# Attention scores as 64x64x64 products in the quarters of the array, and state products of two heads side by side

## The chip, the cores and the metric

The kernel runs on one core of one Trainium2 chip. A time is the device time of one execution in microseconds (us). The engines have short names: PE is TensorE (its weight loads are PEld), DVE is VectorE, ACT is ScalarE, POOL is GpSimd, and SP is SyncE, which here issues the DMAs.

## The reference

One layer of a diffusion backbone: a SwiGLU feed-forward with half a residual, a mixer of two head groups, and a second such feed-forward, for 1024 latent tokens and 256 context tokens of width 1024. Nine vectors per sample (adaLN) shift, scale and gate the stages. The change lies in the first head group, a gated linear attention (GLA) over chunks of 64 tokens that runs in both directions:

```python
GLA_HEADS = 4; GLA_DK = 64; GLA_DV = 128; GLA_CHUNK = 64
def step(s, xs):                                  # one chunk; s is the state
    qc, kc, vc, gc = xs
    b = jnp.cumsum(gc, axis=2)
    rel = b[:, :, :, None, :] - b[:, :, None, :, :]
    decay = jnp.exp(jnp.where(lower, rel, -jnp.inf))
    scores = jnp.einsum('bhid,bhjd,bhijd->bhij', qc, kc, decay)
    o = (jnp.einsum('bhij,bhjv->bhiv', scores, vc)
         + jnp.einsum('bhid,bhdv->bhiv', qc * jnp.exp(b), s))
    ...
s, o = lax.scan(step, s0, ...)                    # forwards, and on flipped tokens backwards
```

Each key feature decays on its own, so a score is no plain product of q and k. The second head group is a gated MLP over chunks of 128 positions (`u * (W_s v + b)`). Both groups are joined and go through one output projection.

## The kernel before

**Blocks.** The 1024 latent tokens are two blocks (`tb`) of 512, each of four tiles of 128. The four heads of the GLA have 64 key features each; two heads lie on the 128 partitions, so `dt` (0, 1) counts pairs of heads and `hp` (0, 1) the half of a pair. A half is 64 partitions.

**Scores by levels.** The kernel works with tiles of 128 tokens, not with chunks of 64. For a pair of tokens whose numbers in a tile differ first in bit `l`, the decay splits into a factor of the query and one of the key, taken at a common border. `level` (L1016) makes the scaled queries and keys of one of seven levels for one pair of heads: `sub` (L1027) on DVE, the exponentials (L897) on ACT, and the product with q and k (L1044) on DVE. `scores` (L1047) takes four products of 128 keys with 128 queries over 64 features into one PSUM bank `sc` (L1056). A stage is a level or the diagonal; it has four such banks, and two blocks have eight stages each: 64 banks. ACT copies the diagonal's banks into the tiles `S` (L1069), and for each level a predicated copy on DVE (L1075) writes those places of a bank that a mask of this level names into `S`. A float32 product is two PE instructions in the trace.

**Outputs of the GLA.** `gla_norm` (L1079) adds three products into a bank `o`: `S` with the values (L1095), and the states that come from the left (L1097) and from the right (L1099) with the scaled queries, each over 64 features. Then come the norm's sums (`st`, L265), a spread over partitions (`bc`, L288) and a product (L1113).

**Order.** The mixer (L1260) records the front, the scores of block 0, the scan of the states (`ds`, L1005), the outputs of block 0, the scores of block 1, 48 sums for the adaLN vectors of the next stage (`ada_part`, L158: a DMA of 256 KB into a tile `ar`, of which there are two, and a sum L168 on DVE against a row `cr`), the projections `vs` (L1135 to L1137) and `ogu` (L356 to L359) that `fill` (L1121) makes, the gated MLP (`mix`, L1221), the outputs of block 1, and the output projection (`wo`), whose sums `x<-wo` DVE adds to the stream (L1312). A scheduler sets each engine's order from these, with simulated costs, under the numbers of buffers that the pools have: three banks `po` for `sc`, `ds`, `o` and `mix`, three banks `pg` for projections, 32 tiles `d` (which hold `S`, `cr`, the inputs of the gated MLP and others), seven tiles `h`. So the projections of `fill`, which depend on none of the scores, stand between them on PE.

Of the kernel before, what the change touches and what calls it, by code (L numbers as in the profile page):

```python
# [9 lines left out]
U8 = mybir.dt.uint8  # L10
I32 = mybir.dt.int32
AF = mybir.ActivationFunctionType
ALU = mybir.AluOpType
# [3 lines left out]
P = 128  # L17
# [5 lines left out]
C_BADA, C_N1, C_N2, C_N3, C_FG, C_BG, C_GG, C_CONV, C_END = 0, 72, 80, 88, 96, 104, 108, 109, 181  # L23


class Layer:
# [72 lines left out]

    def mixer_consts(self):  # L100
        nc, a = self.nc, self.a
        b = self.cp.tile([P, 7 * P + 512], U8, name="bytes", tag="bytes")
        self.masks, self.reset = b[:, :7 * P], b[:, 7 * P:]
        nc.vector.tensor_copy(self.masks, self.load(a["masks"], 7 * P)[:, :7 * P])
# [942 lines left out]
    def scores(self, qk, tp, hp):  # L1047

        ps = self.po("sc")
# [7 lines left out]
        return ps.rearrange("p (h i) -> p h i", i=P)  # L1057

    def gla(self, tb):

        nc = self.nc
        hv = lambda t: t.rearrange("p (h i) -> p h i", i=P)
        S = {}
        for hp in range(2):
            t = self.d("S")
            S[0, hp], S[1, hp] = t[:, :512], t[:, 512:]
# [12 lines left out]
    def gla_norm(self, tb, S, qe):  # L1079

        nc = self.nc
        on, sqs = {}, {}
        st = self.pn("st")
        for hp in range(2):
            r = slice(hp * 64, hp * 64 + 64)
            pos = []
            for dt in range(2):
                po = self.po("o")
                for t in range(4):
                    i = 4 * tb + t  # L1090
                    ts = slice(t * P, (t + 1) * P)
                    c = (2 * (t % 2) + dt) * P
                    sf = self.state(2, 1) if i == 0 else self.state((i - 1) // 4, (i - 1) % 4)
                    sb = self.state(2, 0) if i == 7 else self.state((i + 1) // 4, (i + 1) % 4)
                    nc.tensor.matmul(po[:, ts], self.v[tb, 2 * dt + hp][:, ts], S[t // 2, hp][:, c:c + P],  # L1095
                                     start=True, stop=False)
                    nc.tensor.matmul(po[:, ts], sf[r, dt * P:dt * P + P], qe[dt][r, t * P:t * P + P],  # L1097
                                     start=False, stop=False)
                    nc.tensor.matmul(po[:, ts], sb[r, 256 + dt * P:256 + dt * P + P],  # L1099
                                     qe[dt][r, 512 + t * P:512 + t * P + P], start=False, stop=True)  # L1100
                pos.append(po)
            for dt in range(2):
                h = 2 * dt + hp
                sqs[h] = self.h("sq")
                nc.scalar.activation(sqs[h], pos[dt], AF.Square)
                on[h] = S[dt, hp]
                nc.scalar.activation(on[h], pos[dt], AF.Identity, scale=self.par[:, C_GG:C_GG + 1])
                self.col_sums(st, h, sqs[h], 512)
        on, sqs = ([d[h] for h in range(4)] for d in (on, sqs))
        y = self.rstd_cols(sqs, 512, 1.0 / 128.0, None, st)  # L1110
        for h in range(4):
            bc = self.spread(y[:, 4 * h:4 * h + 4], 4)
            nc.vector.tensor_tensor(out=on[h], in0=on[h], in1=bc, op=ALU.mult)  # L1113
        return on


# [123 lines left out]
    def gla_out(self, on, tb):  # L1240
        dst = self.act_tiles()
        for h in range(4):
            og = self.og[h][:, tb * 512:tb * 512 + 512]
            self.nc.vector.tensor_tensor(out=og, in0=og, in1=on[h], op=ALU.mult)
            self.hilo(og, dst[h])
        return dst

# [174 lines left out]
def pack(i):  # L1422
    import numpy as np

    c = np.ascontiguousarray
# [8 lines left out]
    o = {}  # L1434
# [10 lines left out]
    m = np.zeros((P, 7, P), np.float32)  # L1445
    for l in range(7):
        b = np.arange(P) >> l
        m[:, l] = (b[:, None] ^ b[None, :]) == 1
    o["masks"] = m.reshape(P, 7 * P)
# [36 lines left out]
```

## Time and profile before

| | |
|---|---|
| median of three runs | 2215.16 us (2211.38 to 2219.64) |
| profiled execution: its time, its span | 2211.94 us, 2210.2 us |
| PE busy | 2074.9 us, 94% of the span |
| DVE busy | 1560.1 us, 71% |
| ACT busy | 828.6 us, 37% |
| mean granted clock of PE | 0.951 of full speed |

Positions below are us from the start of the span. The mixer's part that the change touches runs from about 1133 (first copy of a diagonal) to 1500 (output projection done); the feed-forwards lie on either side. A busy PE is one whose instructions overlap in the records; it may be at half its clock, which the clock's column tells.

### The profile page before, as it was taken

Reading aid. Unit: us, or ns where it says so; the run is one execution under the profiler, and the core shown is the slowest. Engines: PE = TensorE matmul, PEld = TensorE weight load, DVE = VectorE, ACT = ScalarE, POOL = GpSimd, SP = SyncE. Lnnn points to the kernel's source line nnn. Section 1 sums busy time; section 2 is a strip of 40 time slices with the busy share of each in tenths; the row PEclk is TensorE's granted clock in tenths of the full one; section 3 lists DMA queues with packets and bytes.
Section 4 is the critical chain, followed back from the end, with each engine's and each line's share of the span. In section 5 each row is a group of like instructions: output and inputs, shape, how many; then the busy total and the mean of one; then the engine's idle time right before and its main releaser. Section 6 shows DMA issues by size and latency. Waiting matters only on the chain.

```text
span 2210.2 us, 27546 instructions
## 1 busy us (share of the span) xinstructions
PE 2074.9 (94%) x10308; PEld 1722.6 (78%) x10308; DVE 1560.1 (71%) x2575; ACT 828.6 (37%) x1311; POOL 420.8 (19%) x245
## 2 busy tenths in 40 slices
PE   6799999999999999698999999996999999989995
PEld 2688888888878888577898787775788888867874
DVE  3976566666565689879877267779777776855587
ACT  3633333334351111275444234326344343441222
POOL 0000000000046565232111100110000000065772
PEclk9799999999999999899999986898999999999997
DMA  7033333233469776401111133541334343468851
GB/s 279 34 115 137 121 119 115 115 136 151 153 249 369 272 293 234 156 11 67 39 58 53 68 128 120 181 156 63 144 136 179 123 181 133 179 259 342 304 196 76
DMA packets 115878, 345.05 MB, mean 156 GB/s; under 512 B 12961, under 2 KB 15777, under 8 KB 115745
## 3 DMA queue, kind: packets, MB, share of 16 engines
q1 hardware_dynamic: 115744, 343.30, 42.2%
q8 instruction: 81, 1.33, 0.2%
q14 instruction: 53, 0.43, 0.1%
HBM read 237.87 MB, written 105.38 MB: 155 GB/s over the span
## 4 chain that ended last, share of the span: by engine, by line
PE 72%; DVE 15%; DMA 5%; POOL 3%; issue 3%; ACT 2%; SPq 0%; POOLq 0%; DVEq 0%; ACTq 0%
PE c L479 14%; PE a L479 13%; PE f L479 13%; PE b L479 7%; DVE acc L741 3%; PE sc L1056 2%; PE gc L526 2%; PE gc L525 2%; PE gc L524 2%; DVE acc L512 2%; DMA ar<-in_wb 1%; PE row L205 1%; PE st L265 1%; PE ogu L358 1%; PE ogu L356 1%
## 5 line engine op out<-in xcount | busy, mean ns | idle before, releaser
L384 POOL TENSOR_TENSOR gl<-raw,gh 128x1024 fp32r<-128x1024 f32 x22 | 54.1, 2461 | 1143.9 <-ACT gh L389 1129.6
L389 ACT ACTIVATE gh<-raw 128x1024 fp32r<-128x1024 f32 x66 | 70.0, 1060 | 198.6 <-PE c L479 83.7
L168 DVE SCALAR_TENSOR_TENSOR junk<-ar,cr 128x512 bf16<-128x512 f32 x160 | 111.9, 700 | 35.4 <-DMA ar<-in_wb 26.3
L393 ACT ACTIVATE sh<-s 128x1024 fp32r<-128x1024 f32 x66 | 69.7, 1057 | 170.8 <-PE a L479 93.2
L429 ACT ACTIVATE hl<-g 128x512 fp32r<-128x512 f32 x110 | 67.5, 626 | 158.8 <-DVE g L512 152.2
L479 PE MATMUL f<-hl,uh 128*128 128x512 f32 x528 | 126.8, 389 | 0.0
L479 PE MATMUL c<-hl,sh 128*128 128x512 f32 x352 | 110.9, 392 | 11.4 <-ACT hl L429 9.2
L479 PE MATMUL a<-hl,gh 128*128 128x512 f32 x352 | 113.6, 400 | 8.1 <-ACT hl L429 5.6
L479 PEld LDWEIGHTS f<-hl,uh 128*128 128x128 f32 x528 | 99.1, 188 | 20.6
L479 PE MATMUL b<-hl,gh 128*128 128x512 f32 x352 | 111.5, 393 | 1.0 <-ACT hl L429 1.0
L479 PE MATMUL f<-hl,th 128*128 128x512 f32 x352 | 110.1, 390 | 1.3 <-ACT hl L429 1.3
L479 PE MATMUL a<-hl,sh 128*128 128x512 f32 x352 | 110.2, 393 | 1.0 <-ACT g L552 1.0
L479 PE MATMUL c<-hl,th 128*128 128x512 f32 x352 | 109.0, 391 | 0.1
L741 DVE SCALAR_TENSOR_TENSOR acc<-z,par,acc 128x945 f32<-128x945 f32 (+2 forms) x64 | 95.5, 1511 | 12.0 <-ACT acc L763 10.9
L512 DVE TENSOR_TENSOR u<-c,u 128x512 f32<-128x512 f32 x44 | 30.3, 689 | 98.4 <-ACT u L562 98.4
L430 DVE TENSOR_TENSOR hl<-g,hl 128x512 fp32r<-128x512 f32 x110 | 76.9, 715 | 32.3 <-ACT hl L429 32.2
L142 POOL TENSOR_TENSOR wl<-raw,wh 128x1024 fp32r<-128x1024 f32 x20 | 52.3, 2614 | 222.5 <-ACT wh L141 213.7
L479 PEld LDWEIGHTS c<-hl,sh 128*128 128x128 f32 x352 | 66.2, 189 | 26.7 <-ACT hl L429 9.8
L384 DVE TENSOR_TENSOR sl<-s,sh 128x1024 fp32r<-128x1024 f32 x44 | 53.9, 1224 | 45.7 <-PE gc L525 21.9
L479 PEld LDWEIGHTS a<-hl,gh 128*128 128x128 f32 x352 | 66.6, 193 | 22.1 <-ACT hl L429 6.1
L512 DVE TENSOR_TENSOR acc<-f,acc 128x512 f32<-128x512 f32 x88 | 60.3, 688 | 28.3 <-PE f L479 23.0
L479 PEld LDWEIGHTS b<-hl,gh 128*128 128x128 f32 x352 | 67.0, 190 | 15.7 <-ACT hl L429 1.8
(330 smaller groups left out, 6211.6 us busy)
## 6 DMA issues: line engine op xcount, KB each, us to landing
hd<-hl SPq DMA_DIRECT2D x154, 512.0 KB, 3.7
hc<-hd SPq DMA_DIRECT2D x154, 512.0 KB, 7.7
ar<-in_wb SPq DMA_DIRECT2D x112, 256.0 KB, 3.1
raw<-in_ff1i SPq DMA_DIRECT2D x44, 512.0 KB, 3.8
raw<-in_ff2i SPq DMA_DIRECT2D x44, 512.0 KB, 4.7
raw<-in_ff1o SPq DMA_DIRECT2D x22, 512.0 KB, 6.2
raw<-in_ff2o SPq DMA_DIRECT2D x22, 512.0 KB, 5.4
raw<-in_wa SPq DMA_DIRECT2D x16, 512.0 KB, 10.0
```

The costliest lines, as they stand in the source:

```text
L142: eng.tensor_tensor(out=lo[:, :n], in0=src[:, :n], in1=hi[:, :n].bitcast(F32), op=ALU.subtract)
L168: i = nc.vector.scalar_tensor_tensor(out=self.junk, in0=w, scalar=1.0, in1=cbc[j], op0=ALU.mult, op1=ALU.mult, accum_out=acc[:, h, dt, j:j ...
L384: sub = lambda o, x, y: eng.tensor_tensor(out=o, in0=x, in1=y, op=ALU.subtract)
L389: nc.scalar.activation(gh, g, AF.Copy)
L393: nc.scalar.activation(sh, s, AF.Copy)
L429: nc.scalar.activation(t[:, :512], src, AF.Copy)
L430: nc.vector.tensor_tensor(out=t[:, 512:], in0=src, in1=t[:, :512].bitcast(F32), op=ALU.subtract)
L479: mm = lambda x, y, start, stop: nc.tensor.matmul(ps, x, y, start=start, stop=stop, skip_group_check=more)
L512: tt = lambda eng, o, x, y, op: eng.tensor_tensor(out=o, in0=x, in1=y, op=op)
L524: nc.tensor.matmul(ps, hi[:, c], mh, start=i == 0, stop=False)
L525: nc.tensor.matmul(ps, hi[:, c], ml, start=False, stop=False)
L741: self.nc.vector.scalar_tensor_tensor(out=o, in0=zv[:, r0 + dr:r1 + dr, c0 + dc:c1 + dc], scalar=self.par[:, tap:tap + 1], in1=o, op0=ALU. ...
```

## The change

Scores are taken in 64x64x64 products. Each tile of 128 tokens is cut into halves of 64, and `scores` takes a stage into two banks, one for each `hp`: the keys' half `h` sets the partitions of the bank (the columns of the array) and `hp` the 64 features (its rows), so that four products that follow one another lie in four quarters. A stage has 32 products of four tiles, two pairs of heads, two halves and two `hp`, 64 PE instructions. Levels 0 to 5 and the diagonal stay within a half: they are kept in compact tiles `Sd` of 8 blocks of 64 columns, one for each `hp`. Level 6 holds every pair across the halves; for it the queries' half is swapped, and no mask is needed. Then eight copies on ACT for each block put `S` together, four from level 6's banks and four from `Sd`. Masks shrink to six of 64 columns. In `gla_norm` the loop over `hp` becomes the innermost, so that two state products in the two row halves follow each other. `S` takes its tiles of pool `d` after the last level instead of before the first.

```diff
-        for t in range(2):
+        ps = [self.po("sc") for _ in range(2)]
+        for t in range(4):
             for dt in range(2):
                 q, k = qk[dt]
-                c = slice((2 * tp + t) * P, (2 * tp + t + 1) * P)
-                o = (2 * t + dt) * P
-                self.nc.tensor.matmul(ps[:, o:o + P], k[r, c], q[r, c], start=True, stop=True)
+                o = (2 * t + dt) * 64
+                for h in range(2):
+                    ck, cq = t * P + h * 64, t * P + (1 - h if cross else h) * 64
+                    for hp in range(2):
+                        r = slice(hp * 64, hp * 64 + 64)
+                        self.nc.tensor.matmul(ps[hp][h * 64:h * 64 + 64, o:o + 64], k[r, ck:ck + 64], q[r, cq:cq + 64],
+                                              start=True, stop=True)
...
-        for (tp, hp), St in S.items():
-            ps = self.scores([(self.q[tb, dt], self.k[tb, dt]) for dt in range(2)], tp, hp)
-            nc.scalar.activation(hv(St), ps, AF.Copy, scale=2.0)
-        for l in range(7):
-            qk = [self.level(tb, l, dt) for dt in range(2)]
-            m = self.masks[:, l * P:(l + 1) * P].unsqueeze(1).to_broadcast([P, 4, P])
-            for (tp, hp), St in S.items():
-                ps = self.scores(qk, tp, hp)
-                nc.vector.copy_predicated(hv(St), m, ps)
+            nc.scalar.activation(Sd[hp], ps[hp], AF.Copy, scale=2.0)
+        for l in range(6):
+            ps = self.scores([self.level(tb, l, dt) for dt in range(2)], False)
+            m = self.masks[:, l * 64:(l + 1) * 64].unsqueeze(1).to_broadcast([P, 8, 64])
+            for hp in range(2):
+                nc.vector.copy_predicated(v(Sd[hp]), m, v(ps[hp]))
+        ps = self.scores([self.level(tb, 6, dt) for dt in range(2)], True)
         self.last_level = self.last_exp
+        S = [self.d("S") for _ in range(2)]
+        for hp in range(2):
+            w = S[hp].rearrange("p (n h i) -> p n h i", h=2, i=64)
+            for h in range(2):
+                r = slice(h * 64, h * 64 + 64)
+                nc.scalar.activation(w[r, :, 1 - h], v(ps[hp])[r], AF.Copy)
+                nc.scalar.activation(w[r, :, h], v(Sd[hp])[r], AF.Copy)
         return S
...
-        for hp in range(2):
-            r = slice(hp * 64, hp * 64 + 64)
-            pos = []
-            for dt in range(2):
-                po = self.po("o")
-                for t in range(4):
+        for dt in range(2):
+            pos = [self.po("o") for _ in range(2)]
+            for t in range(4):
...
+                for dr, x in ((0, sf), (1, sb)):
+                    for hp in range(2):
+                        r = slice(hp * 64, hp * 64 + 64)
+                        c = dr * 512 + t * P
+                        nc.tensor.matmul(pos[hp][:, ts], x[r, dr * 256 + dt * P:dr * 256 + dt * P + P],
+                                         qe[dt][r, c:c + P], start=False, stop=dr == 1)
```

How the scheduler orders it shows at three places. The first is PE in the scores of block 0, where the kernel before puts banks of four products (`sc`) between projections (`vs`). Before:

```order
L1135 MATMUL vs_10497<-wh_10409,y_7644 128x256
L1056 MATMUL sc_9123<-x_9109 128x128
L1056 MATMUL sc_9123<-x_9116 128x128
L1056 MATMUL sc_9123<-x_9109 128x128
L1056 MATMUL sc_9123<-x_9116 128x128
L1136 MATMUL vs_10497<-wl_10410,y_7644 128x256
```

Now, the end of the stage in banks 9109 and 9110, and a piece of one of the next stage's banks (9159) behind it:

```order
L1060 MATMUL sc_9109<-x_9102 64x64
L1060 MATMUL sc_9110<-x_9102 64x64
L1145 MATMUL vs_10621<-wl_10618,y_7644 128x256
L1146 MATMUL vs_10621<-wh_10617,y_7648 128x256
L1060 MATMUL sc_9159<-x_9145 64x64 x2
L1060 MATMUL sc_9159<-x_9152 64x64 x2
L1060 MATMUL sc_9159<-x_9145 64x64 x2
L1060 MATMUL sc_9159<-x_9152 64x64 x2
L1060 MATMUL sc_9159<-x_9145 64x64 x2
L1060 MATMUL sc_9159<-x_9152 64x64 x2
L1060 MATMUL sc_9159<-x_9145 64x64 x2
L1060 MATMUL sc_9159<-x_9152 64x64 x2
```

In the first of these stages the two banks alternate, so all four quarters are in turn; in the next only one bank is free, and 16 products of one `hp` run by themselves, in the two column halves of one row half. Of the 16 stages nine go wholly or mostly as the first, seven as the second.

The second place is PE at the end of block 1's scores. Before, the last bank of scores is followed by the outputs:

```order
L1056 MATMUL sc_9994<-x_9962 128x128
L1056 MATMUL sc_9994<-x_9969 128x128
L1095 MATMUL o_11089<-S_9712,v_8484 128x128
L1097 MATMUL o_11089<-b_7871,st_9301 128x128
L1099 MATMUL o_11089<-b_7871,st_9302 128x128
L1095 MATMUL o_11089<-S_9712,v_8484 128x128
```

Now one bank of outputs stands before the last scores, and projections of `fill` behind them:

```order
L1102 MATMUL o_11297<-S_10198,v_8484 128x128
L1108 MATMUL o_11297<-b_7871,st_9407 128x128
L1108 MATMUL o_11297<-b_7871,st_9403 128x128
L1060 MATMUL sc_10165<-x_10157 64x64
L1060 MATMUL sc_10165<-x_10150 64x64 x2
L1060 MATMUL sc_10165<-x_10157 64x64 x2
L358 MATMUL ogu_11161<-y_7646,wh_11157 128x512
L359 MATMUL ogu_11161<-y_7642,wl_11158 128x512
```

In all, 44 instructions of `ogu` that stood before block 1's outputs now stand between them and behind. The state products (now L1108) of two heads stand next to each other in one of four groups of outputs only (block 0, first pair of heads); in the three others one bank follows the other.

The third place is DVE in the output projection, where sums of adaLN (L168) stand between the additions to the stream (L1312, now L1322). Before:

```order
L1312 SCALAR_TENSOR_TENSOR x_11336<-wo_11509,mods,x_11336 128x512
L168 SCALAR_TENSOR_TENSOR junk,acc_10113<-ar_10132,cr_10008 128x512
L1159 TENSOR_TENSOR al_11641<-og_11354,ah_11640 128x512
L1312 SCALAR_TENSOR_TENSOR x_11334<-wo_11528,mods,x_11334 128x512
L1312 SCALAR_TENSOR_TENSOR x_11336<-wo_11542,mods,x_11336 128x512
L168 SCALAR_TENSOR_TENSOR junk,acc_10113<-ar_10135,cr_10008 128x512
L1312 SCALAR_TENSOR_TENSOR x_11338<-wo_11561,mods,x_11338 128x512
```

Now:

```order
L1322 SCALAR_TENSOR_TENSOR x_11536<-wo_11618,mods,x_11536 128x512
L168 SCALAR_TENSOR_TENSOR junk,acc_10270<-ar_10286,cr_10216 128x512
L168 SCALAR_TENSOR_TENSOR junk,acc_10270<-ar_10289,cr_10216 128x512
L1322 SCALAR_TENSOR_TENSOR x_11538<-wo_11637,mods,x_11538 128x512
L168 SCALAR_TENSOR_TENSOR junk,acc_10270<-ar_10292,cr_10216 128x512
L168 SCALAR_TENSOR_TENSOR junk,acc_10270<-ar_10295,cr_10216 128x512
L1322 SCALAR_TENSOR_TENSOR x_11540<-wo_11651,mods,x_11540 128x512
```

The 48 sums need the row `cr`, which now takes its tile of pool `d` after `S`. Before, 34 of them stood ahead of the first addition to the stream, 20 of these among the levels of block 1. Now none stands ahead of the end of these levels, 18 stand between it and the first addition, and 30 behind that, two after each of some 15 additions.

## Rows read from the trace of the kernel before

**Rows 1.** The page: busy time, share and instructions of each engine.
```profile
PE 2074.9 (94%) x10308; PEld 1722.6 (78%) x10308; DVE 1560.1 (71%) x2575; ACT 828.6 (37%) x1311; POOL 420.8 (19%) x245
```
**Rows 2.** The chain that ended last: its shares, then pieces (start, us, what).
```profile
PE 72%; DVE 15%; DMA 5%; POOL 3%; issue 3%; ACT 2%; SPq 0%; POOLq 0%; DVEq 0%; ACTq 0%
```
**Rows 3.** The same chain in the mixer's middle, block 0 and block 1.
```profile
1158.94 1.09 PE sc L1056 x8
1160.03 0.31 PE vs L1137
1160.34 0.12 PE vs L1135
...
1351.61 1.74 PE sc L1056 x8
...
1411.79 0.77 DVE x L1312
...
1565.70 2.72 PE b L479 x12
```
**Rows 4.** Windows: us, busy PE, PEld, DVE, ACT, POOL (instructions), clock, DMA, GB/s.
```profile
1136.00:1200.00 64.00, 64.00 (x445) 56.17 (x445) 52.37 (x90) 21.18 (x32) 6.81 (x3) 1.00 0.17 55
1200.00:1236.00 36.00, 36.00 (x286) 28.38 (x284) 11.61 (x32) 17.69 (x29) 4.74 (x2) 1.00 0.14 52
1236.00:1270.00 34.00, 34.00 (x159) 26.84 (x159) 11.40 (x28) 7.46 (x11) 3.61 (x1) 0.85 0.25 85
1270.00:1353.00 83.00, 79.41 (x411) 65.77 (x409) 62.77 (x138) 37.36 (x56) 5.48 (x4) 0.79 0.38 124
1353.00:1390.00 37.00, 37.00 (x130) 29.01 (x131) 14.88 (x36) 8.89 (x19) 2.79 (x2) 0.50 0.30 94
1390.00:1412.00 22.00, 18.93 (x167) 14.81 (x163) 19.83 (x48) 5.04 (x8) 0.00 (x0) 0.93 0.41 127
1412.00:1500.00 88.00, 85.99 (x390) 71.14 (x391) 69.20 (x125) 29.31 (x43) 14.75 (x10) 0.98 0.58 200
```
**Rows 5.** Timeline of PE: start, us, instruction, its tile of the array, count.
```profile
1231.70 2.84 PE L1005 MATMUL ds<-v,kt 128*64 128x128 f32 x48
...
1250.74 0.49 PE L1095 MATMUL o<-S,v 128*128 128x128 f32 x2
...
1251.80 0.49 PE L1095 MATMUL o<-S,v 128*128 128x128 f32 x2
...
1255.61 0.37 PE L1097 MATMUL o<-b,st 64*128 64x128 f32 x1
1255.62 0.37 PE L1099 MATMUL o<-b,st 64*128 64x128 f32 x1
...
1290.62 1.93 PE L1056 MATMUL sc<-x,qk 64*128 64x128 f32 x18
...
1353.28 0.79 PE L1095 MATMUL o<-S,v 128*128 128x128 f32 x2
...
1355.16 0.79 PE L1095 MATMUL o<-S,v 128*128 128x128 f32 x2
```
**Rows 6.** Instructions by line: duration min/median/max in ns, first and last start.
```profile
L1075 DVE COPY_PREDICATED S<-bytes,sc x56: 716/733/751, 1138.2 to 1353.4; 128x512 f32<-128x512 uint8 x56
...
L1069 ACT ACTIVATE S<-sc x8: 588/597/597, 1133.0 to 1283.3; 128x512 f32<-128x512 f32 x8
```
**Rows 7.** A window in the levels of block 1, columns as in rows 4.
```profile
1330.00:1335.00 5.00, 4.11 (x18) 3.52 (x17) 5.00 (x11) 2.39 (x5) 0.00 (x0) 0.50 0.18 56
```
**Rows 8.** Windows of the adaLN sums alone (L168): two records per sum.
```profile
1270.00:1353.00 83.00, 14.40 (x40) 0.79 0.38 124
...
1412.00:1500.00 88.00, 11.90 (x28) 0.98 0.58 200
```
**Rows 9.** Timeline of DVE in the output projection: two of eight sums.
```profile
1448.21 0.68 DVE L168 SCALAR_TENSOR_TENSOR junk<-ar,cr 128x512 bf16<-128x512 f32 x1
...
1462.91 0.69 DVE L168 SCALAR_TENSOR_TENSOR junk<-ar,cr 128x512 bf16<-128x512 f32 x1
```

More of the change, by code (lines that the diff above doesn't have):

```diff
@@ L101, in mixer_consts @@
         nc, a = self.nc, self.a
-        b = self.cp.tile([P, 7 * P + 512], U8, name="bytes", tag="bytes")
-        self.masks, self.reset = b[:, :7 * P], b[:, 7 * P:]
-        nc.vector.tensor_copy(self.masks, self.load(a["masks"], 7 * P)[:, :7 * P])
+        b = self.cp.tile([P, 6 * 64 + 512], U8, name="bytes", tag="bytes")
+        self.masks, self.reset = b[:, :6 * 64], b[:, 6 * 64:]
+        nc.vector.tensor_copy(self.masks, self.load(a["masks"], 6 * 64)[:, :6 * 64])
         nc.vector.memset(self.reset, 1)
@@ L1045, in level, with scores @@
         return x[:, :512], x[:, 512:]
[L1047 to L1051 removed]
+    def scores(self, qk, cross):
+        ps = [self.po("sc") for _ in range(2)]
+        for t in range(4):
             for dt in range(2):
                 q, k = qk[dt]
[L1054 to L1057 removed]
+                o = (2 * t + dt) * 64
[5 more added lines that the diff above has]
+                                              start=True, stop=True)
+        return ps
@@ L1059, in gla @@
     def gla(self, tb):
         nc = self.nc
-        hv = lambda t: t.rearrange("p (h i) -> p h i", i=P)
-        S = {}
+        v = lambda t: t.rearrange("p (n i) -> p n i", i=64)
+        Sd = [self.h("Sd") for _ in range(2)]
+        ps = self.scores([(self.q[tb, dt], self.k[tb, dt]) for dt in range(2)], False)
         for hp in range(2):
-            t = self.d("S")
-            S[0, hp], S[1, hp] = t[:, :512], t[:, 512:]
-        for (tp, hp), St in S.items():
-            ps = self.scores([(self.q[tb, dt], self.k[tb, dt]) for dt in range(2)], tp, hp)
-            nc.scalar.activation(hv(St), ps, AF.Copy, scale=2.0)
@@ L1083, in gla_norm @@
         st = self.pn("st")
-        for hp in range(2):
-            r = slice(hp * 64, hp * 64 + 64)
-            pos = []
-            for dt in range(2):
-                po = self.po("o")
-                for t in range(4):
[L1090 to L1095, printed above, removed]
-                                     start=True, stop=False)
[L1097 to L1102, printed above, removed]
+        for dt in range(2):
+            pos = [self.po("o") for _ in range(2)]
+            for t in range(4):
+                i = 4 * tb + t
+                ts = slice(t * P, (t + 1) * P)
+                c = (2 * t + dt) * P
+                sf = self.state(2, 1) if i == 0 else self.state((i - 1) // 4, (i - 1) % 4)
+                sb = self.state(2, 0) if i == 7 else self.state((i + 1) // 4, (i + 1) % 4)
+                for hp in range(2):
+                    nc.tensor.matmul(pos[hp][:, ts], self.v[tb, 2 * dt + hp][:, ts], S[hp][:, c:c + P],
+                                     start=True, stop=False)
+                for dr, x in ((0, sf), (1, sb)):
+                    for hp in range(2):
+                        r = slice(hp * 64, hp * 64 + 64)
+                        c = dr * 512 + t * P
+                        nc.tensor.matmul(pos[hp][:, ts], x[r, dr * 256 + dt * P:dr * 256 + dt * P + P],
+                                         qe[dt][r, c:c + P], start=False, stop=dr == 1)
+            for hp in range(2):
@@ L1112, in gla_norm @@
             bc = self.spread(y[:, 4 * h:4 * h + 4], 4)
-            nc.vector.tensor_tensor(out=on[h], in0=on[h], in1=bc, op=ALU.mult)
+            nc.vector.tensor_tensor(out=on[h], in0=on[h], in1=bc.rearrange("p (t i) -> p t i", i=P), op=ALU.mult)
         return on
@@ L1243, in gla_out @@
             og = self.og[h][:, tb * 512:tb * 512 + 512]
-            self.nc.vector.tensor_tensor(out=og, in0=og, in1=on[h], op=ALU.mult)
+            ov = og.rearrange("p (t i) -> p t i", i=P)
+            self.nc.vector.tensor_tensor(out=ov, in0=ov, in1=on[h], op=ALU.mult)
             self.hilo(og, dst[h])
@@ L1444, in pack @@
     o["ident"] = np.eye(P, dtype=np.float32)
[L1445 to L1449, printed above, removed]
+    m = np.zeros((P, 6, 64), np.float32)
+    for l in range(6):
+        m[:, l] = ((np.arange(P)[:, None] % 64) >> l) ^ (np.arange(64)[None, :] >> l) == 1
+    o["masks"] = m.reshape(P, 6 * 64)
     wa = i["w_ada"][0]
```

7 lines of the change are left out of this document (4 added, 3 removed).

## The prediction

> **What bounds the kernel now.** I read the page's busy shares first, then the chain of waits, then windows by stage, and last the timelines of PE and DVE. PE is busy for 94% of the span [rows 1], and 72% of the chain that ended last is PE [rows 2]. So time saved on PE counts where PE ends the waits, and work taken from DVE or ACT counts only where these do. Around the change the chain runs, in block 0's levels, through banks of scores and `vs` projections in turn. In block 1 it comes to the last bank of scores, which ends at 1351.61 + 1.74 = 1353.35 and which I call t0; at 1411.79 it reaches the first addition to the stream [rows 3].
>
> The windows tell the stages apart [rows 4]. In block 0's levels (1136 to 1200) PE is busy all 64 us at full clock, DVE 52.37: PE bounds. The next 36 us belong to keys, states and projections, which the change leaves alone. The outputs of block 0 (1236 to 1270) are PE at a mean clock of 0.85. In block 1's levels (1270 to 1353) PE is busy 79.41 of 83 us but at 0.79, with DVE at 62.77: both count. Then come 37 us of PE at exactly half clock, 22 us in which DVE is nearly full (19.83), and 88 us of output projection in which PE is busy 85.99.
>
> **The change part by part.** *Scores on PE.* 18 instructions of the old kind last 1.93 us, 107 ns each [rows 5]. A bank of eight takes 1.09 us in the chain, 0.23 more than 8 x 107 ns, and the first projection behind it takes 0.31 instead of 0.12 us [rows 3]. So a run of scores between other products costs 0.23 + 0.19 = 0.42 us for the two changes of shape. Before, 512 instructions stand in 43 runs: 512 x 0.107 + 43 x 0.42 = 73 us. Now 1024 stand in 29 runs. No row shows a 64x64 product. The nearest is `ds`, which uses the two column halves in turn with 128 moving columns: 48 in 2.84 us, 59 ns each [rows 5], half of a full-width one. I take half of 59, since only 64 columns move: 1024 x 29.6 ns = 30 us, and 29 x 0.42 = 12: 42 us, so -30. One bound is four quarters at once in every stage: two products in the two row halves can start 10 ns apart [rows 5], which would halve 29.6 again, 15 + 12 = 27 us, -46. Seven of the 16 stages run one `hp` by itself, where row halves can't help; therefore I stay with the column halves alone. The other bound is that a 64-wide product costs what a 128-wide one of `ds` costs: 1024 x 59 ns + 12 = 73 us, and PE gains nothing.
>
> The Trainium skill speaks against thin products: "TensorEngine Tiling (Array Packing)", Instruction Overhead, says that each matmul carries about 60 cycles and that one should not split a dimension that is already small. Read at 2.4 GHz that is 25 ns, an estimate of 26 us for 1024, which leaves my 30 standing and excludes the end with -46; read at 1.2 GHz it is 50 ns and 51 us, close to the bound without gain. No row here shows a product denser than 59 ns, so the trace can't yet tell.
>
> *DVE.* 56 predicated copies of 0.733 us [rows 6] become 24: -23.5 us, 11.7 in each block. In block 0 this lies beside PE and is worth nothing by itself; it lowers DVE there to 41 us, so PE stays the bound after it has lost 15 (to 49). In block 1 it is worth something, since there PE waits for DVE at times (DVE busy 5.00 of 5 us, [rows 7]).
>
> *ACT.* 16 new copies, at most 0.6 us each as a full copy of a bank is [rows 6], less four of the diagonal: +7 us on an engine with 21 to 37 us in the levels [rows 4], hidden, but for those between the last scores of a block and its first output. Two to eight copies can stand there, 1.2 to 4.8 us; I take four, 2.4, in each block: +5 in all.
>
> *State products.* Three products of an output take 1.06 us (1250.74 to 1251.80, [rows 5]), about 0.35 each. Ten pairs in block 0 now stand side by side and save one of two: -3. Elsewhere the order leaves them one bank after the other: 0.
>
> *Sums and projections that move.* 20 adaLN sums (14.40 us with their reads, 0.72 each [rows 8]) leave block 1's levels, and 44 products of `ogu` too. At 2.72 us for 12 such products [rows 3] these are 10 us of PE, which come back behind t0.
>
> *By stage.* Block 0's levels: of the 15 us that PE loses I count 12, because a stage now starts only when both pairs of heads are scaled, and PE will wait for a few. Outputs of block 0: -3. Block 1's levels: -12 as in block 0, and -8 of the 10 us of moved projections: -20. Copies on the path: +5. So t0 comes about 30 earlier. Behind t0: four more sums ahead of the first addition to the stream, 0.72 each: +3; the moved projections +10; and, because these are dense products between the outputs, I let half of what 37 us at half clock lose (18.5) come back: -9. Together +4. In the output projection there are 30 sums instead of 14. An addition (0.77 [rows 3]) and two sums need 0.77 + 2 x 0.72 = 2.2 us of DVE for 2.72 us of PE, so DVE hides them. With 14 sums PE lost 2.0 of 88 us [rows 4]; by proportion 30 lose 4.3, +2; with some waits for the rows' DMA I take +4. The upper bound is below, as a rival. Sum: -30 + 4 + 4 = -22 from the profiled 2211.94 us: 2190 us. (This execution lies 3.2 us under the median of the runs shown, 2215.16, and within their spread of 8.)
>
> **The rivals.** *Thin products don't overlap* (59 ns each, the rule above). For: no row shows better. Against: `ds` gets half of the full-width time by using halves of the columns. PE then gains nothing in either block, block 0 keeps its 64 us; block 1 keeps some 8 by DVE's relief and the moved projections, which come back behind t0; the copies add 5. Time 2204 to 2214, about 2210.
>
> *All four quarters at once, and the clock stays up.* For: two row halves start 10 ns apart [rows 5], and nine stages alternate as this needs. Against: seven stages don't. Scores fall by 46 instead of 30, of which DVE (41 us in block 0) lets most through, and block 1's 0.79 and the 0.50 behind it rise. Another 10 to 30 us: 2160 to 2180, of which the lower part is outside my own range.
>
> *The output projection gives it back.* Eight sums stand from 1448.21 to 1462.91, 2.1 us from one to the next, three times what one lasts, since `ar` has two tiles and DVE waits for the DMA [rows 9]. Two sums for each of 15 additions at this pace are 4.2 us instead of 2.72: +22 instead of +4, and SP's queue, where these loads wait for their tile, holds back what is queued behind them. For: the order puts 30 sums there. Against: PE lost only 2 us with 14. Time 2205 to 2222.
>
> *The clock falls in the levels: slower than before.* In 1330 to 1335 PE runs short banks of scores between waits for DVE, busy 4.11 of 5 us, and its clock is 0.50 [rows 7]; behind t0 it runs outputs at 0.50 and three products take 1.88 us (1353.28 to 1355.16, [rows 5]) instead of 1.06. If PE, now quicker with the scores than DVE with the levels, does so in block 0 too, the 49 us of full-clock work that are left there need more than the old 64 as soon as the mean clock is below 49/64 = 0.77; at 0.60 they take 82, +18, and block 1 with about 47 us of work at 0.55 takes 85, as before. With the copies, +5, and the moved work, +10, that is 2222 to 2245. For: the rows just named. Against: block 0 has projections to fill every gap, and its clock was 1.00 with DVE at 82%.
>
> **How the numbers follow.** Chances: forecast 0.50; no overlap 0.14; four quarters 0.14; the projection gives it back 0.12; clock 0.10. Some 0.5% of this time (11 us) is what a measurement can tell from no change, so faster means below 2204 and slower above 2226. Faster: 0.50 less 0.03, and 0.14: 0.61, with a little of the two cases near 2205, 0.63. Slower: most of the clock's 0.10 and some unlisted mishap: 0.12. Same: the rest, 0.25. The forecast's own range is 2172 to 2204. The range for 8 in 10 leaves out the lowest part of the four quarters and most of the clock's case: 2162 to 2222.
>
> **What would show it.** Right: banks of `sc` of 32 instructions in about 0.95 us where one `hp` runs alone; block 0's levels 10 to 14 us shorter at clock 1.00; 24 predicated copies; t0 near 1323; first addition to the stream near 1385; PE still over 95% busy in the output projection. If a product costs 59 ns, the first rival holds; at 15 ns in the stages where banks alternate, the second. Waits of DVE for `ar` over 10 us in the output projection would show the third, a granted clock under 0.77 in block 0's levels the fourth. I would be wrong in kind if t0 came no earlier although the scores on PE shrank: then DVE's or ACT's chain through the levels, not PE, was what ended there.

## The result, and the profile after

The changed kernel takes 2186.16 us (median of four runs, 2178.66 to 2190.47) against 2214.68 before (the three runs of the table and a fourth): a ratio of 0.9864, 95% interval 0.9846 to 0.9882, some 28 us less. The profiled execution took 2185.07 us, 26.9 less than that of before. So the forecast of 2190 and its range held. The way there was another: two of its terms were far too small, and they have opposite signs.

The page, answering to [rows 1, 2]:

```profile
PE 2016.1 (92%) x10820; PEld 1669.9 (76%) x10820; DVE 1541.3 (71%) x2543; ACT 832.8 (38%) x1322; POOL 420.2 (19%) x245
...
PE 67%; DVE 17%; DMA 6%; issue 6%; ACT 3%; POOL 1%; SPq 0%; POOLq 0%; DVEq 0%; ACTq 0%
```

PE has 59 us less to do, twice what the time fell; its share of the chain went from 72% to 67%. To see where, the mixer is cut at the same events in both kernels: first score, first `ds`, first output, first score of block 1, last score (t0), first and last addition to the stream. Before, at these cuts (columns as in [rows 4]):

```profile
1111.40:1202.70 91.30, 90.04 (x654) 81.06 (x655) 71.31 (x117) 38.43 (x70) 11.75 (x5) 1.00 0.16 53
1202.70:1235.30 32.60, 32.60 (x267) 25.80 (x267) 10.91 (x30) 15.38 (x24) 2.65 (x2) 1.00 0.14 50
1235.30:1269.60 34.30, 34.30 (x161) 26.91 (x159) 11.74 (x30) 8.16 (x13) 3.61 (x1) 0.86 0.25 85
1269.60:1353.30 83.70, 80.11 (x413) 66.25 (x412) 63.43 (x140) 37.66 (x56) 5.48 (x4) 0.79 0.38 124
1353.30:1411.80 58.50, 55.57 (x291) 43.68 (x290) 34.21 (x84) 13.63 (x27) 2.79 (x2) 0.66 0.33 104
1411.80:1500.30 88.50, 86.35 (x392) 71.47 (x393) 69.68 (x126) 29.31 (x43) 14.75 (x10) 0.98 0.58 201
```

And after:

```profile
1118.10:1181.40 63.30, 59.63 (x850) 56.52 (x850) 58.02 (x101) 36.87 (x69) 4.71 (x2) 0.95 0.15 48
1181.40:1213.00 31.60, 31.60 (x262) 25.00 (x262) 12.75 (x31) 17.04 (x28) 7.09 (x3) 1.00 0.24 76
1213.00:1245.80 32.80, 32.80 (x175) 26.47 (x173) 10.00 (x30) 9.87 (x17) 2.39 (x1) 0.88 0.09 33
1245.80:1304.00 58.20, 56.36 (x695) 45.28 (x695) 43.80 (x81) 24.04 (x35) 7.64 (x5) 0.92 0.17 56
1304.00:1384.60 80.60, 52.71 (x346) 43.05 (x344) 51.48 (x115) 40.60 (x69) 8.44 (x5) 0.81 0.63 221
1384.60:1475.50 90.90, 84.94 (x359) 66.80 (x360) 64.24 (x136) 18.02 (x27) 9.41 (x7) 0.98 0.53 177
```

Block 0's levels are 28 us shorter and block 1's 25.5. The stretch from t0 to the first addition is 22 longer, and in it PE now stands idle for 80.60 - 52.71 = 27.9 us, before for 2.9. (The lead-in to the first score, which the change does not touch, ends at 1118.1 instead of 1111.4; over all the profiles taken here it scatters from 1110.5 to 1118.3.)

The scores on PE by themselves, in block 0's and block 1's levels of before, then in all of the changed kernel (L1060 is their line now):

```profile
1111.40:1202.70 91.30, 33.29 (x256) 28.70 (x256) 1.00 0.16 53
...
1269.60:1353.30 83.70, 42.81 (x256) 36.75 (x256) 0.79 0.38 124
```

```profile
1118.10:1304.00 185.90, 31.52 (x1024) 27.22 (x1024) 0.94 0.16 52
```

33.3 + 42.8 = 76.1 us became 31.5: -44.6. PE's timeline shows how (start, us, instruction, count). The first row is a stage in which the banks alternate, the second one `hp` alone:

```profile
1155.62 1.32 PE L1060 MATMUL sc<-x 64*64 64x64 f32 x60
1159.57 1.15 PE L1060 MATMUL sc<-x 64*64 64x64 f32 x32
...
1281.23 1.04 PE L1060 MATMUL sc<-x 64*64 64x64 f32 x56
1282.20 0.50 PE L356 MATMUL ogu<-y,wh 128*128 128x512 f32 x1
```

From 1281.23 to the next product at 1282.20, 56 alternating instructions take 0.97 us, 17 ns each; the 60 of the first row take 1.24 us up to the next instruction, 21 ns each. The 32 of one `hp` take 1.15 us to the last one's end. (Prices here are for one instruction; a float32 product is two.)

What holds back the first addition (DVE's timeline, with the idle time before an instruction and its releaser in brackets; then PE's waits from 1304 to 1390: us in total, times, longest):

```profile
1311.67 0.69 DVE L168 SCALAR_TENSOR_TENSOR junk<-ar,cr 128x512 bf16<-128x512 f32 x1 [14.30 <-ACT cr L183]
...
1365.31 0.69 DVE L168 SCALAR_TENSOR_TENSOR junk<-ar,cr 128x512 bf16<-128x512 f32 x1 [2.47 <-DMA ar<-in_wb]
...
1370.21 2.50 DVE L1254 TENSOR_TENSOR og<-og,S 128x512 f32<-128x512 f32 x4 [4.20 <-ACT og L1246]
...
1383.90 0.15 DVE L154 TENSOR_TENSOR mods<-acc,par 128x8 f32<-128x8 f32 x1
1383.98 0.68 DVE L168 SCALAR_TENSOR_TENSOR junk<-ar,cr 128x512 bf16<-128x512 f32 x1
...
1384.59 2.06 DVE L1322 SCALAR_TENSOR_TENSOR x<-wo,mods,x 128x512 f32<-128x512 f32 x3
```

```profile
PE wo L356 <- DVE x L1322: 23.3, 1, 23.3
```

The row `cr` is loaded right behind the last score; its DMA is issued at 1304.2. The first sum runs at 1311.67. The vector `mods` that gates the output projection needs 16 sums and is ready at 1383.90, and the first addition follows within a microsecond. PE waits 23.3 us for it. The sum at 1365.31 is the 14th. The last two, at 1373.22 and 1377.93, and the vector itself stand in DVE's order among the products of the GLA's outputs with their gates (`og`), for whose inputs DVE has to wait.

### The profile page after: what moved, and what is told of

Same layout as the page of the kernel before. It is cut to its first block, busy times and chain, and to the rows that moved or that the text cites. A ratio compares the mean times of both kernels' runs of the same rounds, so it can differ in the third digit from the quotient of the medians.

```text
span 2183.3 us, 28555 instructions
## 1 busy us (share of the span) xinstructions
PE 2016.1 (92%) x10820; PEld 1669.9 (76%) x10820; DVE 1541.3 (71%) x2543; ACT 832.8 (38%) x1322; POOL 420.2 (19%) x245
## 4 chain that ended last, share of the span: by engine, by line
PE 67%; DVE 17%; DMA 6%; issue 6%; ACT 3%; POOL 1%; SPq 0%; POOLq 0%; DVEq 0%; ACTq 0%
PE c L479 15%; PE a L479 14%; PE f L479 14%; PE b L479 7%; DVE acc L741 4%; DVE acc L512 2%; DMA ar<-in_wb 2%; PE gc L526 2%; PE gc L525 2%; PE gc L524 2%; DMA hc<-hd 2%; PE row L205 1%; DVE junk L168 1%; DVE hl L430 1%; DVE x L625 1%
## 5 line engine op out<-in xcount | busy, mean ns | idle before, releaser
L168 DVE SCALAR_TENSOR_TENSOR junk<-ar,cr 128x512 bf16<-128x512 f32 x160 | 112.6, 704 | 63.7 <-DMA ar<-in_wb 45.1
L741 DVE SCALAR_TENSOR_TENSOR acc<-z,par,acc 128x945 f32<-128x945 f32 (+2 forms) x64 | 95.5, 1512 | 12.3 <-ACT acc L763 11.3
L356 PE MATMUL wo<-ah,wo 128*128 128x512 f32 x128 | 52.1, 408 | 30.0 <-DVE x L1322 28.1
L479 PEld LDWEIGHTS a<-hl,sh 128*128 128x128 f32 x352 | 67.2, 191 | 16.0 <-ACT g L552 1.3
```

The source lines that it names most:

```text
L168: i = nc.vector.scalar_tensor_tensor(out=self.junk, in0=w, scalar=1.0, in1=cbc[j], op0=ALU.mult, op1=ALU.mult, accum_out=acc[:, h, dt, j:j ...
L356: m = nc.tensor.matmul(out, a_, xh[k], start=(i == 0), stop=False)
L479: mm = lambda x, y, start, stop: nc.tensor.matmul(ps, x, y, start=start, stop=stop, skip_group_check=more)
L741: self.nc.vector.scalar_tensor_tensor(out=o, in0=zv[:, r0 + dr:r1 + dr, c0 + dc:c1 + dc], scalar=self.par[:, tap:tap + 1], in1=o, op0=ALU. ...
```

## The experiments

Each is an edit of the changed kernel unless it says otherwise, with four runs (ten where it is one of the kernel before). Times are to be held against 2186.2 (changed) and 2214.7 (before).

**Row halves apart.** The loop over `hp` goes outermost in `scores`:

```diff
+        for hp in range(2):
+            r = slice(hp * 64, hp * 64 + 64)
             for t in range(4):
...
-                    for hp in range(2):
-                        r = slice(hp * 64, hp * 64 + 64)
```

> The changed kernel with the loop over hp outermost in a stage of scores: the 32 instructions of one row half run before those of the other, so only the column halves alternate. Theory (the quarters work side by side: four products start in about 58 ns where the banks alternate, two where they don't): a product starts every 29 ns in all stages, the scores take about 14 us more on PE (33 to 47), and as PE ends most waits in the levels the time is 2192 to 2200 us. Rival (DVE's and ACT's work on the levels sets their pace, PE's time is hidden): within 3 us of the changed kernel, 2183 to 2189.

2182.5 us (ratio to before 0.9846, 0.9830 to 0.9862). This is 0.5 us outside the rival's range and far from the theory's. The scores' time on PE rose only to 34.15 us, by 2.6:

```profile
1115.10:1298.70 183.60, 34.15 (x1020) 31.00 (x1022) 0.93 0.17 54
```

```profile
1159.65 1.79 PE L1060 MATMUL sc<-x 64*64 64x64 f32 x64
```

The expectation of 14 more counted all stages, but seven of the 16 had no alternating halves to lose; nine stages would make 8 (9 x 64 x 14.5 ns). Two quarters at a time also cost a little less than expected: the 64 instructions of the second row take 1.72 us up to the next one at 1161.37, 27 ns each. So they do nearly as well as the mixture, and the 3 us are worth nothing.

**The row early.**

```diff
+        row = self.d("cr")
+        self.cond_row(0, slice(0, 1024), row)
         g1 = self.gla(1)
         q1 = [self.queries(1, dt) for dt in range(2)]
-        row = self.d("cr")
-        self.cond_row(0, slice(0, 1024), row)
```

> The changed kernel with the row cr, which the 48 adaLN sums need, loaded before the scores of block 1 are recorded; nothing else moved by hand. By the order the sums then stand between the blocks' levels, where DVE has room. Theory (the late row and its 16 sums of the vector that gates the output projection hold back the first addition to the stream, with SP's queue behind them): the stretch from the last score to the first addition falls from 81 to about 60 us and the time to 2165 to 2174. Rival (loads and activations of the gates end this stretch whatever the sums do): 2182 to 2188, and DVE, 44 of 58 us busy in block 1, shows no gain either.

2182.4 us (0.9847, 0.9822 to 0.9873): only 4 us, which is in the rival's range but not for the rival's reason, since the stretch to the first addition did fall to 52.4. The keys, the outputs of block 0 and the levels of block 1 took 9, 16 and 9 us more, and their clock fell:

```profile
1181.00:1221.30 40.30, 36.27 (x269) 28.40 (x270) 26.02 (x63) 18.78 (x30) 7.56 (x3) 0.92 0.58 178
1221.30:1270.30 49.00, 45.54 (x192) 36.95 (x191) 30.72 (x81) 10.95 (x17) 5.41 (x2) 0.72 0.47 143
1270.30:1337.30 67.00, 62.69 (x697) 50.83 (x698) 48.91 (x100) 22.76 (x34) 5.59 (x4) 0.83 0.36 116
1337.30:1389.70 52.40, 47.59 (x301) 40.83 (x298) 26.21 (x60) 26.50 (x50) 2.50 (x2) 0.73 0.49 181
```

From 1181 to 1275 DVE waited 28.5 us in 25 pieces for rows of `ar`:

```profile
DVE junk L168 <- DMA ar<-in_wb: 28.5, 25, 2.4
```

So with the row early the wait ahead of the addition is gone, and 40 sums are no better among the keys and the outputs of block 0. Whether a late row must bring that wait is another question; the runs below answer it.

**The sums early too.** The loop of the 48 sums moves along with the row.

```diff
         self.cond_row(0, slice(0, 1024), row)
+        for ch in (5, 6, 7):
+            for h in range(2):
+                for dt in range(NK):
+                    self.ada_part(ch, dt, h, [row[:, h * 512:h * 512 + 512]])
         g1 = self.gla(1)
```

> As the kernel with the early row, with the 48 sums recorded there too. Theory: the row's place decides, not the record of the sums; the same time as with the row alone within 4 us. Rival: sums that go first in the record take DVE and SP from the outputs of block 0, and it is slower than with the row alone by 5 to 10.

2181.0 us (0.9845): the same as with the row alone. The place of the row decides.

**Copies twice.**

```diff
                 nc.vector.copy_predicated(v(Sd[hp]), m, v(ps[hp]))
+                nc.vector.copy_predicated(v(Sd[hp]), m, v(ps[hp]))
```

> The changed kernel with each of the 24 predicated copies done twice, 17.6 us more on DVE. Theory (PE ends most waits, with DVE close behind in block 0: 58 of 63 us busy, 44 of 58 in block 1): block 0 grows by 4 to 7, block 1 by 0 to 3, time 2189 to 2196. Rival (DVE's chain sets the pace of the levels, and its 23.5 us fewer are the gain): the whole 17.6 comes back, 2200 to 2206.

2190.1 us (0.9877, 0.9859 to 0.9895): 4 of the 17.6 us reach the end, a time in the theory's range. The stages are not the theory's: block 0's levels grew by 16 us and block 1's by 0.8, while the stretch from the last score to the first addition fell from 80.6 to 62.0 and the output projection took 10 more.

```profile
1112.30:1191.60 79.30, 74.07 (x906) 68.01 (x906) 69.69 (x113) 41.68 (x76) 10.36 (x5) 0.94 0.17 58
...
1315.00:1377.00 62.00, 57.91 (x311) 45.69 (x305) 35.54 (x96) 29.83 (x53) 0.00 (x0) 0.64 0.53 182
```

The scheduler, with more work on DVE, put 53 instructions of `ogu` (15.0 us) back into block 0's levels, where the kernel before had 58 and the changed kernel has none; behind the last score it left none of 44. So the run doesn't show what DVE's work costs with all else in its place.

**States one by one.** In `gla_norm` the loop over `hp` goes around the loop over `t`, so that one bank of outputs follows the other.

```diff
+            for hp in range(2):
+                r = slice(hp * 64, hp * 64 + 64)
                 for t in range(4):
...
-                for hp in range(2):
```

> The changed kernel with the loop over hp outside in each group of outputs, so that no two state products of different row halves stand side by side. Theory (ten pairs side by side in block 0 save about 0.15 to 0.3 us each): 2186 to 2190 us, 1 to 3 more than the changed kernel, in block 0's outputs alone. Rival (the order of the outputs sets more, by the clock or the banks): over 5 us either way.

2175.5 us (0.9816, 0.9786 to 0.9846): 11 faster, the rival's size, against the theory. Block 0's outputs did get slower, by 3.8 us and at a lower clock (32.80 us at 0.88 in the changed kernel):

```profile
1208.10:1244.70 36.60, 36.60 (x163) 28.62 (x161) 10.00 (x30) 8.33 (x14) 2.39 (x1) 0.81 0.08 30
```

But the first addition came at 1364.4 instead of 1384.6 and the last at 1464.2 instead of 1475.5:

```profile
L1321 DVE SCALAR_TENSOR_TENSOR x<-wo,mods,x x32: 736/746/752, 1364.4 to 1464.2; 128x512 f32<-128x512 f32 x32
```

The vector `mods` is ready at 1364.18, 62 us after the DMA of its row at 1302.0, against 80 us in the changed kernel; all 16 sums stand ahead of the `og` products here. Whether the 11 us are the outputs' order or this place of the sums, the run with both edits below tells.

**Sums late in the old kernel.** The kernel before, with an ordering edge from the last level of block 1 to every sum:

```diff
-                    self.ada_part(ch, dt, h, [row[:, h * 512:h * 512 + 512]])
+                    self.ada_part(ch, dt, h, [row[:, h * 512:h * 512 + 512]], self.last_level)
```

> The kernel before with its 48 adaLN sums held behind the last level of block 1 by an ordering edge; nothing else. Theory (20 sums that leave the levels come back as waits of DVE for their rows ahead of the output projection, as in the changed kernel, where this stretch grew by 22 us): block 1's levels 5 to 12 us shorter, the stretch to the first addition 15 to 30 longer, time 2220 to 2232. Rival (the sums hide behind PE there, and the stretch in the changed kernel grew by its moved projections): 2205 to 2214.

2220.6 us (1.0027, 1.0013 to 1.0041), at the theory's lower end, with the loss in another place:

```profile
1277.00:1353.60 76.60, 75.20 (x411) 62.80 (x411) 53.56 (x105) 36.84 (x54) 5.17 (x4) 0.83 0.25 78
1353.60:1413.80 60.20, 57.77 (x293) 46.10 (x291) 34.83 (x87) 14.34 (x29) 2.49 (x2) 0.63 0.36 114
1413.80:1512.80 99.00, 89.07 (x390) 70.30 (x390) 78.25 (x158) 29.30 (x43) 14.68 (x10) 0.98 0.63 216
```

The levels gain 7 us, and the output projection with its 29 sums takes 99 instead of 88.5, PE idle for 10 of them: the pace that the third rival named, at half its price. The stretch to the first addition grew by 1.7 us only, from 58.5 to 60.2, and not by 15 to 30, although all 48 sums now start behind the last level. Their row was there by then (its DMA was issued at 1253.5), and the 16 sums again stand ahead of the `og` products.

**Quarter by quarter.** Products that follow each other lie in the same quarter:

```diff
+        for hp in range(2):
+            r = slice(hp * 64, hp * 64 + 64)
+            for h in range(2):
                 for t in range(4):
...
                     for dt in range(2):
...
-                for h in range(2):
...
-                    for hp in range(2):
-                        r = slice(hp * 64, hp * 64 + 64)
```

> The changed kernel with the scores of a stage taken quarter by quarter (hp, then h outermost), so that products which follow each other lie in the same quarter and can't run side by side: a product every 58 ns, 1024 of them 60 us instead of about 26, 30 to 34 us more on PE. Theory (PE's time on the scores is the gain): 25 to 34 us come back, 2210 to 2220. Rival (DVE sets the pace of the levels, 58 of 63 us in block 0, and PE has room, as the run with the row halves apart suggests): 8 to 15 come back, 2193 to 2201.

2183.0 us (0.9855, 0.9829 to 0.9880): nothing came back, less than either expected. The edit did what it should: 32 instructions take 1.90 us, 59 ns each (124 in one run, from 1299.88, take 6.19 us, 50 ns each), and the scores 59.65 us, 28 more:

```profile
1159.64 1.90 PE L1060 MATMUL sc<-x 64*64 64x64 f32 x32
```

```profile
1113.10:1306.00 192.90, 59.65 (x1024) 56.60 (x1024) 0.95 0.14 45
```

Where they went, by stage:

```profile
1113.10:1182.50 69.40, 69.40 (x848) 66.79 (x848) 56.71 (x101) 38.32 (x72) 4.73 (x3) 1.00 0.14 45
...
1245.00:1305.90 60.90, 60.90 (x648) 55.07 (x647) 40.81 (x81) 21.08 (x31) 12.82 (x3) 0.86 0.11 37
1305.90:1374.30 68.40, 63.91 (x397) 51.05 (x395) 44.24 (x105) 32.20 (x58) 6.18 (x4) 0.88 0.58 195
```

The levels take 9 us more in both blocks together, now with PE busy throughout, and projections move from there into the stretch ahead of the first addition, where PE's idle time falls from 27.9 to 4.5 us. Up to the last score 7 us do come back. Behind it they are won again, partly by the sums: `mods` is ready at 1362.15, 57 us after its row's DMA instead of 80, and no longer holds the first addition at 1374.3. So this run does not tell what the scores cost where the sums stay put; the one with spread sums and quarters comes closer.

**Sums spread.** The row and the 16 sums of the gate (vector 5) go ahead of `self.gla(1)`; the other 32 are tied to additions, one behind each of the first 16 and two behind each of the next eight:

```diff
+        for h in range(2):
+            for dt in range(NK):
+                self.ada_part(5, dt, h, [row[:, h * 512:h * 512 + 512]])
         g1 = self.gla(1)
...
-                self.wo_add(w, bm[tb], dt, tb)
+                self.late_sum(row, self.wo_add(w, bm[tb], dt, tb))
...
-                self.wo_add(ws[dt], ag[tb], dt, tb)
+                add = self.wo_add(ws[dt], ag[tb], dt, tb)
+                for _ in range(0 if tb else 2):
+                    self.late_sum(row, add)
...
+    def late_sum(self, row, add):
+        ch, h, dt = self.late.pop(0)
+        self.ada_part(ch, dt, h, [row[:, h * 512:h * 512 + 512]], add)
```

> The changed kernel with the row cr and the 16 sums of the gating vector recorded before block 1's scores, and the other 32 tied to the 24 first additions to the stream, one or two behind each. Theory (what the early row lost was DVE's waits for 43 rows between the blocks; 16 cost less, and the wait ahead of the first addition is gone): keys and outputs of block 0 5 to 10 us longer, the stretch to the first addition 22 to 28 shorter, time 2168 to 2175. Rival (whatever PE no longer waits, it loses to a lower granted clock in the outputs, as with the early row): 2178 to 2184.

2168.7 us (0.9789, 0.9764 to 0.9814), as the theory had it, with 35 us less in the stretch to the first addition where it had 22 to 28, and more in the projection. From t0 to the first addition 45.9 us remain, PE never idle, at 0.87 instead of the 0.73 of the early row; the projection pays 7:

```profile
1312.80:1358.70 45.90, 45.90 (x321) 38.62 (x319) 28.28 (x60) 27.11 (x51) 3.27 (x2) 0.87 0.66 238
1358.70:1456.60 97.90, 86.55 (x369) 68.64 (x367) 76.88 (x149) 29.61 (x43) 14.81 (x10) 0.98 0.54 173
```

**Spread sums and quarters**, the two edits above together:

> The kernel with the spread sums (2168.7 us) with its scores taken quarter by quarter, 25 us more on PE as measured. Theory (in the changed kernel this cost nothing because PE stood idle for 28 us ahead of the first addition, which waits for 16 sums that can't start before the last level; where that wait is gone, time follows PE's work): 2184 to 2194. Rival (DVE's work on the levels hides the scores in any case): 2166 to 2174.

2177.1 us (0.9831, 0.9806 to 0.9857): 8.4 over the spread kernel, between the two (the four times of one lie apart from those of the other, the intervals of the ratios just overlap). Without the wait the scores' time does count, but only a third of it.

**Spread sums and a third tile.**

```diff
-    BUFS = dict(raw=2, ar=2, w=6, m=8, d=32, sv=3, h=7, pg=3, po=3, pn=2)
+    BUFS = dict(raw=2, ar=3, w=6, m=8, d=32, sv=2, h=7, pg=3, po=3, pn=2)
```

> The kernel with the spread sums with three tiles ar instead of two, and two tiles sv instead of three to make room. Theory (in its output projection, 98 us with PE idle for 11, DVE waits for the DMA of the rows): 5 to 10 us less, 2159 to 2164. Rival (the sums stand in the order behind additions, and DVE waits for PE there; or the tile that sv gives up costs as much): 2166 to 2172.

2163.2 us (2158.6 to 2171.8; 0.9771, 0.9738 to 0.9803). The median lies in the theory's range, but the projection falls by 1.2 us only, to 96.7, with PE idle for 8.0 instead of 11.3, and the interval overlaps that of the spread kernel: a gain over it is not shown. This is the lowest median of all versions, about 1% under the changed kernel.

**Spread sums and states one by one**, again two edits together:

> The kernel with the spread sums with its outputs as in the run with the states one by one. Theory (that run was 11 us faster than the changed kernel because its 16 sums ended 15 us earlier, by their place in the order, while block 0's outputs took 4 us more): without the wait for the sums only the 4 us are left, 2170 to 2175. Rival (the order of the outputs is better by itself): 2156 to 2163.

2170.0 us (0.9794, 0.9766 to 0.9821), the theory's side within the noise: with the sums out of the way the outputs' order is worth nothing either way. So the 11 us of the run alone came from the place of the sums.

**Quarters and copies.** Both costs put back in the changed kernel:

> The changed kernel with both costs put back at once: scores quarter by quarter (25 us more on PE, which alone cost nothing: 2183) and each predicated copy done twice (17.6 us more on DVE, which alone cost 4: 2190). Theory (a level ends with the later of PE and DVE, so that either alone is covered by the other, and the change gained because it lightened both): much more than the sum of the two, 2198 to 2210. Rival (each hides for a reason of its own): the sum, 2183 to 2192.

2193.8 us (0.9911, 0.9890 to 0.9931): 7.6 over the changed kernel, where the two alone make -3.2 and +3.9. This lies between the rival's range and the theory's. That the two cover each other is not shown: PE is busy for 82.2 of 82.3 us of block 0's levels and all 63.9 of block 1's, 51 instructions of `ogu` stand in block 0's again, and the stretch to the first addition is 62.1 us as with the copies alone.

## Why the prediction was right, and where it was not

*Scores on PE: the mechanism right, the size too small.* The 73 us were right (76.1 measured, some of it at half clock). The 42 were not: 31.5. I took two quarters at a time for all stages and the old price for a change of shape. With two at a time throughout, the run with the row halves apart took 34.2 us, so some 8 of the 10.5 us lie in these prices (29.6 ns for each of 64 instructions and 0.42 us for their run make 2.3 us; 1.72 measured). Only 2.6 lie in the nine stages that had four at a time, as the second rival said, at 17 to 21 ns an instruction. The first rival is excluded for this order; quarter by quarter it is just what happens, 59 ns an instruction. The Trainium skill's "TensorEngine Tiling (Array Packing)", Instruction Overhead, would allow one matmul every 25 ns or slower (an estimate from its 60 cycles at 2.4 GHz, read as a bound on the next start); the 17 ns of the trace go below that, so the rule is no bound for products in different quarters.

*Block 0's levels: -28 instead of -12.* PE is idle 3.7 us there, as I had allowed. The scores alone fell from 33.3 to 15.1 us. I had missed that 58 instructions of `ogu`, 14 us, were no longer done there. They went into block 1's levels, which gained 15, and behind t0, whose 44 I did count.

*Outputs of block 0: -1.5 instead of -3.* Side by side the state products save: those of both heads for one tile and pair take 0.65 us (8 instructions from 1228.06 to 1228.71), and in the run with the states one by one those of one head alone take 0.64 (4 from 1222.92 to 1223.56). There the whole stretch took 3.8 us more.

*Block 1's levels with the copies: -25.5, where -20 and some of the +5 stood.* The 24 predicated copies and the moved sums came as counted. The -8 for 44 products of `ogu` that leave this stage did not: it has 118 of their instructions where it had 103, since the 44 come from block 0. What made up for it is the scores, 26.3 us less here (42.8 became 16.5) where I had 12.

*Behind t0: the step that failed.* I priced four more sums at 3 us of DVE and the stretch at +4; it was +22, of which 25 are new idle time of PE. The sums' length was not the cost, but when they can start and where they stand. Their row `cr` is loaded when the last level is done, the first addition can't run before 16 sums have passed, and the last of these stand among the `og` products, which wait for loads of their own. The chain from 1304.2 to 1383.9 is 80 us long and PE has work for 53 of them. Moved early, the row takes the wait away (the stretch falls to 52), and so do the spread sums (-17.5 us in all). But the late row alone is not enough for it: with the row just as late, `mods` came 56 to 62 us after the row's DMA in four runs (states one by one, copies twice, quarter by quarter, quarters and copies), in each of which the 16 sums stood ahead of the `og` products. Held against the states one by one (62.5 us from the last score to the first addition), 18 of the 22 us are this place in DVE's order. The third rival had the mechanism, waits for rows and a queue behind them, but placed it in the output projection, and gave it 0.12. The sign that I named for it came there: DVE waits 20.1 us for `ar` (5.1 before) and PE stands idle for 6.0 us instead of 2.2. Yet that stretch grew by 2.4 us only.

*The moved projections, +10, and the clock, -9.* Nearly as said. The 44 instructions take 10.6 us. PE's other work up to the first addition takes 42.2 us instead of 55.6, at a granted clock of 0.81 instead of 0.66. Behind the dense products the outputs start at full clock (1.00 from 1310 to 1324). PE is busy 3.8 of the 5 us from 1319 to 1324, waits 1.4 us for the norm's squares, and runs eight sums of one column; from 1327 to 1331 the clock is 0.50:

```profile
1310.56 0.49 PE L1102 MATMUL o<-S,v 128*128 128x128 f32 x2
...
1311.61 0.49 PE L1102 MATMUL o<-S,v 128*128 128x128 f32 x2
...
1324.22 1.05 PE L265 MATMUL st<-ones,sq 128*128 128x1 f32 x8 [1.44 <-ACT sq L1113]
...
1327.45 0.79 PE L1102 MATMUL o<-S,v 128*128 128x128 f32 x2
...
1329.32 0.79 PE L1102 MATMUL o<-S,v 128*128 128x128 f32 x2
```

Three products take 1.05 us in the first pair of rows with `S` and 1.87 in the second. The fourth rival fell: the levels ran at 0.95 and 0.92.

So the sum was right by luck: two misses met. Up to t0 the gain was 56 us from the first score on (91.3 + 32.6 + 34.3 + 83.7 became 63.3 + 31.6 + 32.8 + 58.2), 26 more than forecast. Behind t0 24.5 us were lost (22.1 and 2.4) where 8 were forecast, 16.5 more. The lead-in took 7 that belong to no step, and the feed-forward behind gave back 2. The first addition came at 1384.6, where I had said 1385, but t0 at 1304 and not at 1323.

What stays open is how the gain divides between PE and DVE in the levels. Putting back 28 us on PE costs nothing at the end, 17.6 on DVE 4, both 7.6; but in each of these runs the projections or the 16 sums moved as well. With the sums spread, the 28 us on PE cost 8.4. No run put back the rest: the last 16 us of the scores (76.1 against 60), eight predicated copies, and the places that the scheduler gives to the projections.

## What to carry to other kernels

Price work that moves by the moment at which its first input can exist, here the load of the row it reads, by what stands ahead of it in its engine's order, and by who waits for its last result; its own length says little. When an engine loses a lot of work, look for the first wait that does not shrink with it: here 25 of PE's 59 us turned into idle time in one place, and a regrouping of 48 small sums, which is no part of the change, was worth another 0.8%.

## What the runs showed of the hardware

These are instructions of 64 rows and 64 columns of float32 with 64 moving columns, at a granted clock of 1.00. One quarter after the other (the run quarter by quarter), they took 59 ns each in a run of 32 and 50 ns in a run of 124. In two quarters in turn (the run with the row halves apart) 64 took 27 ns each. Alternating over all four (the changed kernel) gave 17 ns over 56 instructions. Four quarters instead of two saved only 2.6 us of 34 here; seven of the 16 stages could not alternate.
